# Storing the first 120 sums of each partition early and the last 8 late, in a row-sum kernel at the end of a stream of loads

## The chip, the cores and the metric

One core of one Trainium2 chip runs the whole program. The metric is the time of one execution on the device in microseconds (us), the median over several executions. The profile is one execution taken by the hardware profiler; its times count from the start of the span. The span leaves out about 2.0 us of the measured time. Engines are TensorE (PE), VectorE (DVE), ScalarE (ACT), GpSimd (POOL) and SyncE (SP), which issues the transfers. A transfer of the kernel has one descriptor (the order to move one piece) for each partition, and the trace shows each piece as a packet. A transfer has landed when the last of the 16 DMA engines has raised its semaphore. The receipt is the time from the end of an engine's last packet to that signal.

## The reference

```python
def setup_inputs():
    batch, seq, dim = 32, 512, 1024
    return {"x": np.abs(np.random.randn(batch, seq, dim)).astype(np.float32) + 1e-6}

def reference(x):
    return np.sum(1.0 / x, axis=-1).astype(np.float32)
```

There are 16384 rows of 1024 numbers. Each of the 128 partitions gets 128 rows, so the result is a tile of 128 partitions by 128 columns of float32: 512 bytes for each partition, 64 KB in all.

## The kernel before

Loads of x (64 MB) stream through a ring of 40 rows. A row is handled as two halves a and b, since 1/a + 1/b = (a + b)/(ab): products on GpSimd or VectorE, reciprocals as exp(-ln) on ScalarE, half sums on TensorE, and the multiplication with the sum over the row on VectorE, whose result goes to one column of `sums`. The last 24 rows follow a fixed order, in which `T119` means "sum of row 119"; `W127` and `X127` handle row 127 on ScalarE alone.

```python
    LAST = 104
    LAST_LOADS = [2] * 1 + [4] * 1 + [2] * 5 + [1] * 8
    ORDER = """
        ... E116 S118 V118 E117 P120 T115 L118+
        P121 S119 T116 E118+ T117 P122 L120+ S122 T118 E120+ D123 L122+ T120
        S123 P124 E122+ T119 D125 S125 L124 T122 L125 P126 T121 E124 S126 E125
        T123 L126 T124 W127 E126 T125 X127 T126
    """
    # ... cut: the pools, the main loop over rows 0 to 103, the loads of the last rows ...
    for op in order:
        # ... cut: the other kinds of operation ...
        elif kind == "X":
            keep(nc.scalar.activation(out=rows, in_=rows, func=Exp, scale=-1.0,
                                      accum_out=sums[:, c : c + 1]))

    nc.sync.dma_start(out=out_v, in_=sums)
```

The transfers are numbered in the order of their issue: 31 loads, then the store as the 32nd. Each signals its completion on one of eight semaphores, used in turn. At its end SyncE waits for eleven semaphores: the eight, and one each of GpSimd, ScalarE and VectorE.

## Time and profile before

| quantity | value |
|---|---|
| time, median of 6 runs (those taken with the changed kernel included) | 169.22 us (169.12 to 169.84) |
| span of the profiled run | 167.1 us |
| the one store: issue, in us from the start | 164.767 |
| issue to last landing | 1.537 us |
| last landing to the end of the span | 0.834 us |

The lines of the page that carry this, and how they are read, stand in the prediction below. One more is needed later, from the view of the program's end (L286): how often SyncE's queue ran a semaphore instruction there, with the shortest, median and longest duration in ns, and when the first and the last began.

```profile
L286 SPq EVENT_SEMAPHORE  x7: 17/28/28, 165.2 to 167.1; - x7
```

Five of these seven are the waits for the eleven semaphores (a drain carries the eleventh), two belong to the barrier, in which the engines wait for one another. The wait for the store is not inside a record here. In these traces a record begins once the first semaphore that the instruction names is there: the fifth instruction names the store's semaphore first and began at 166.320, 0.016 us after the landing.

### The profile page before, as it was taken

Reading aid. Unit: us, or ns where it says so; the run is one execution under the profiler, and the core shown is the slowest. Engines: PE = TensorE matmul, PEld = TensorE weight load, DVE = VectorE, ACT = ScalarE, POOL = GpSimd, SP = SyncE. Lnnn points to the kernel's source line nnn. Section 1 sums busy time; section 2 is a strip of 40 time slices with the busy share of each in tenths; the row PEclk is TensorE's granted clock in tenths of the full one; section 3 lists DMA queues with packets and bytes.
Section 4 is the critical chain, followed back from the end, with each engine's and each line's share of the span. In section 5 each row is a group of like instructions: output and inputs, shape, how many; then the busy total and the mean of one; then the engine's idle time right before and its main releaser. Section 6 shows DMA issues by size and latency. Waiting matters only on the chain.

```text
span 167.1 us, 1139 instructions
## 1 busy us (share of the span) xinstructions
PE 108.6 (65%) x204; PEld 43.0 (26%) x204; DVE 135.6 (81%) x272; ACT 133.9 (80%) x137; POOL 130.2 (78%) x73
## 2 busy tenths in 40 slices
PE   0007946193864919179471935926999996998990
PEld 0003321040321303033221302402444442433430
DVE  0001797979979798998979897898699999998994
ACT  3002888979788797878979785999899999999994
POOL 1007969698895969979696985999999997999630
PEclk9999999969789699957999696985899999999999
DMA  6999999999999999999999999999999999999910
GB/s 204 423 439 439 431 439 416 447 408 463 408 441 431 439 439 431 431 418 439 416 439 431 447 396 416 427 422 431 433 423 414 433 420 422 418 416 410 409 64 18
DMA packets 4614, 67.23 MB, mean 402 GB/s; under 512 B 512, under 2 KB 640, under 8 KB 1664
## 3 DMA queue, kind: packets, MB, share of 16 engines
q1 hardware_dynamic: 4608, 67.18, 94.7%
q14 instruction: 5, 0.04, 0.1%
q8 instruction: 1, 0.02, 0.0%
HBM read 67.11 MB, written 0.07 MB: 402 GB/s over the span
## 4 chain that ended last, share of the span: by engine, by line
DMA 67%; POOL 12%; ACT 7%; issue 6%; DVE 4%; SPq 1%; PE 1%; ACTq 1%; POOLq 0%
DMA ring<-in_x_dram 67%; POOL pr L158 12%; ACT pr L230 3%; DVE ring L109 2%; ACT pr L236 2%; DVE pr L109 2%; SPq L139 1%; ACT r L236 1%; PE bb L99 1%; ACT pr L169 1%; ACT ring L248 1%; ACT r L174 1%; ACTq L286 1%; DVE pr L221 0%; DVE sums L109 0%
## 5 line engine op out<-in xcount | busy, mean ns | idle before, releaser
L158 POOL TENSOR_TENSOR pr<-ring 128x1024 f32<-128x1024 f32 (+1 forms) x52 | 107.2, 2102 | 26.6 <-DMA ring<-in_x_dram 24.2
L99 PE MATMUL s<-ring,ident 128*128 128x512 f32 x172 | 89.5, 669 | 5.8 <-DVE sums L109 5.5
L169 ACT ACTIVATE pr<-pr 128x1024 f32<-128x1024 f32 x52 | 54.7, 1051 | 27.8 <-POOL pr L158 27.1
L109 DVE CUSTOM_DVE_ANT_1 pr<-ring,r 128x1024 f32<-128x1024 f32 x40 | 48.8, 1221 | 10.2 <-ACT r L174 9.8
L109 DVE CUSTOM_DVE_ANT_1 ring<-ring,r 128x1024 f32<-128x1024 f32 x44 | 53.4, 1216 | 0.0
L99 PEld LDWEIGHTS s<-ring,ident 128*128 128x128 f32 x172 | 36.8, 218 | 58.7 <-issue 41.2
L99 PE MATMUL b<-ring,ident 128*128 128x512 f32 x26 | 19.0, 820 | 46.8 <-DMA ring<-in_x_dram 46.8
L174 ACT ACTIVATE r<-pr 128x1024 f32<-128x1024 f32 x36 | 37.0, 1028 | 1.1
L109 DVE CUSTOM_DVE_ANT_0 pr<-pr,s 128x512 f32<-128x512 f32 x43 | 27.9, 682 | 0.0
L212 POOL TENSOR_TENSOR pr<-ring 128x512 f32<-128x512 f32 (+1 forms) x15 | 22.3, 1500 | 4.2 <-DMA ring<-in_x_dram 2.5
L147 DVE TENSOR_TENSOR pr<-ring,b 128x512 f32<-128x512 f32 x13 | 8.9, 685 | 18.5 <-PE b L99 18.5
L99 PEld LDWEIGHTS b<-ring,ident 128*128 128x128 f32 x26 | 5.2, 238 | 56.2 <-DMA ring<-in_x_dram 37.8
L179 ACT ACTIVATE pr<-pr 128x1024 f32<-128x1024 f32 x16 | 16.9, 1058 | 0.5
L230 ACT ACTIVATE pr<-pr 128x1024 f32<-128x1024 f32 (+1 forms) x14 | 12.4, 899 | 0.5 <-DVE pr L221 0.3
L109 DVE DVE_READ_ACCUMULATOR2_ANT sums<- 128x1 f32 x127 | 10.5, 83 | 0.0
L236 ACT ACTIVATE r<-pr 128x1024 f32<-128x1024 f32 (+1 forms) x8 | 6.4, 806 | 0.1
L236 ACT ACTIVATE pr<-pr 128x1024 f32<-128x1024 f32 (+1 forms) x7 | 6.0, 863 | 0.1
L99 PE MATMUL bb<-ring,ident 128*128 128x512 f32 x6 | 3.4, 644 | 2.0 <-DMA ring<-in_x_dram 1.2
L221 DVE TENSOR_TENSOR pr<-ring,bb 128x512 f32<-128x512 f32 x3 | 2.1, 685 | 0.3 <-PE bb L99 0.2
L99 PEld LDWEIGHTS bb<-ring,ident 128*128 128x128 f32 x6 | 0.9, 188 | 4.5 <-DMA ring<-in_x_dram 2.8
L70 ACT ACT_TABLE_LOAD x1 | 1.3, 1283 | 0.7 <-PEq L275 0.7
L214 DVE TENSOR_TENSOR pr<-ring 128x512 f32<-128x512 f32 x2 | 1.4, 687 | 0.0
(9 smaller groups left out, 3.2 us busy)
## 6 DMA issues: line engine op xcount, KB each, us to landing
ring<-in_x_dram SPq DMA_DIRECT2D x10, 4096.0 KB, 37.1
ring<-in_x_dram SPq DMA_DIRECT2D x7, 2048.0 KB, 35.7
ring<-in_x_dram SPq DMA_DIRECT2D x6, 1024.0 KB, 30.8
ring<-in_x_dram SPq DMA_DIRECT2D x8, 512.0 KB, 14.4
out_dram<-sums SPq DMA_DIRECT2D x1, 64.0 KB, 1.5
```

Of the source, the lines that this page charges most:

```text
L99: i = nc.tensor.matmul(bank, lhsT=ident, rhs=half, start=k == 0, stop=k == len(halves) - 1,)
L109: i = nc.vector.tensor_tensor_reduce(out=row if out is None else out, in0=row, in1=fac, scale=S, scalar=0.0, op0=mult, op1=plus, accum_out ...
L139: keep(nc.sync.dma_start(out=xt, in_=x_v[:, c0 : c0 + n, :]))
L147: i = nc.vector.tensor_tensor(out=pr[:, j, :], in0=xt[:, q + j, :H], in1=b, op=mult)
L158: i = nc.gpsimd.tensor_tensor(out=pr[:, v:, :], in0=xc[:, v:, :H], in1=xc[:, v:, H:], op=mult)
L169: keep(nc.scalar.activation(out=pr, in_=pr, func=Ln, scale=S))
L174: nc.scalar.activation(out=r, in_=pr[:, e:, :], func=Exp, scale=-1.0)
L179: keep(nc.scalar.activation(out=r, in_=r, func=Exp, scale=-1.0))
L212: keep(nc.gpsimd.tensor_tensor(out=pr, in0=a, in1=b, op=mult))
L221: nc.vector.tensor_tensor(out=pr[:, 0, :], in0=a[:, 0, :], in1=bs[c], op=mult)
L230: keep(nc.scalar.activation(out=pr, in_=pr, func=Ln, scale=S))
L236: keep(nc.scalar.activation(out=r, in_=pr, func=Exp, scale=-1.0))
```

## The change

The intent is to take most of the store's bytes off the end: 120 of 128 columns are complete some 5 us before the last one, so they can leave while the last rows are still computed, and only 4 KB are left for the end.

```diff
+    STORED = 120
...
+    left = set(range(LAST, F))
     for op in order:
...
-
-    nc.sync.dma_start(out=out_v, in_=sums)
+        if kind in "TX":
+            left.discard(c)
+            if c < STORED and min(left) >= STORED:
+                keep(
+                    nc.sync.dma_start(out=out_v[:, :STORED], in_=sums[:, :STORED])
+                )
+
+    assert not left
+    nc.sync.dma_start(out=out_v[:, STORED:], in_=sums[:, STORED:])
```

## The prediction

> **What bounds the kernel now.** I read the page's first lines first, then the slices, then the tail in the timeline and the waits of SyncE's queue, because the change touches nothing but how the sums leave the chip.
>
> ```profile
> span 167.1 us, 1139 instructions
> DMA  6999999999999999999999999999999999999910
> GB/s 204 423 439 439 431 439 416 447 408 463 408 441 431 439 439 431 431 418 439 416 439 431 447 396 416 427 422 431 433 423 414 433 420 422 418 416 410 409 64 18
> DMA 67%; POOL 12%; ACT 7%; issue 6%; DVE 4%; SPq 1%; PE 1%; ACTq 1%; POOLq 0%
> ```
>
> For 38 of 40 slices the loads of x run at some 420 GB/s, and the chain of waits puts 67% of the span on them. That part is not touched. The last two slices (a slice is 4.2 us) are a tail: the last row's arithmetic, then the one store of all sums, then the end of the program. What the change can move is there alone. The timeline of the tail:
>
> ```profile
> 158.66 0.68 DVE L109 CUSTOM_DVE_ANT_0 pr<-pr,s 128x512 f32<-128x512 f32 x1
> 159.27 0.08 DVE L109 DVE_READ_ACCUMULATOR2_ANT sums<- 128x1 f32 x1
> ...
> 164.56 0.19 ACT L251 ACTIVATION_READ_ACCUMULATOR ring<-ring 128x1 f32 x1
> 164.59 0.08 DVE L109 DVE_READ_ACCUMULATOR2_ANT sums<- 128x1 f32 x1
> 164.77 0.34 SPq L260 DMA_DIRECT2D out_dram<-sums  x1
> ```
>
> The last sum of VectorE (row 126) is there at 164.59 + 0.08 = 164.67, the one of ScalarE (row 127) at 164.56 + 0.19 = 164.75 (164.74 unrounded), and the store is issued at 164.77, hence behind ScalarE. The first two lines are the sum of row 119: in the program's order it is the last of rows 0 to 119, so 120 columns are there at 159.35. Between are 5.4 us in which a store could leave. Then the list of DMA issues and the waits of SyncE's queue:
>
> ```profile
> out_dram<-sums SPq DMA_DIRECT2D x1, 64.0 KB, 1.5
> SPq L260 <- DVE sums L109: 13.0, 1, 13.0
> SPq L286 <- DMA out_dram<-sums: 0.9, 1, 0.9
> ```
>
> From issue to landing the store takes 1.5 us, and the end of the program (L286) waits 0.9 us of them. So the exposed end is 164.77 to 167.14, some 2.4 us. I took it apart from the trace's records of single packets and of SyncE's sequencer (us from the start): issue 164.767 to 165.110 (0.343); first packet 165.606; 128 packets of 512 bytes, about 27 ns each, and the 16 small ones that raise the semaphore, the last ending at 165.965; last landing seen at 166.304; SyncE's next instruction at 166.320; last instruction of the barrier ends at 167.138. Measured time (169.21) is 2.1 us above the span and stays so.
>
> **What the Trainium skill says.** (1) "DMA: Bandwidth & Descriptors", section "Anatomy of one DMA", puts a fixed cost of about 2 us on a transfer, most of it the receipt of the write and nearly none of it its bytes. The trace agrees in kind: of 1.54 us (164.767 to 166.304) only 0.36 are packets; 0.84 lie before the first and 0.34 behind the last. (2) The same page, "Measured", has 0.68 us of DMA busy time for 4 KB and 0.95 us for 64 KB (loads, issued by GpSimd), a difference of 0.27; those are just the sizes of the late store and of the old one, but here all 64 KB took 0.36, so I size the gain from the packets instead. (3) Its "Specifications" say that pieces under 512 bytes make the DMA read, modify and write. The old store has 512 bytes for each partition, the new ones 480 and 32. No record of before shows this. (4) "Queues, rings and completion order" says that an engine takes the descriptors of one ring in order; so the early store, issued by SyncE like the loads, goes behind the loads that are still queued. The last data packet of the loads ends at 160.95; the trace of before has nothing to test this.
>
> **The change part by part.** Comparing the order of instructions on each engine, PE, DVE, ACT and POOL have the same instructions with the same waits; SyncE has one transfer more. In particular DVE's later sums do not wait for the early store, since it reads other columns.
>
> *Early store, 120 columns.* It waits for the sum of row 119 (159.35) and for an old load; issue takes some 0.34 us, first packet at the earliest 159.4 + 0.84 = 160.2, behind the loads by 161.0, landed by about 161.6, more than 3 us ahead of the late store's issue. The DMA is idle from 161 on. All of it lies beside VectorE's and ScalarE's arithmetic: cost 0. Gain also 0 of itself, since another store is still to come.
>
> *Late store, 8 columns.* It waits for the same last sums of ScalarE and VectorE, so it is issued at 164.77 as before. It has still 128 descriptors, one for each partition. Issue is the same whatever their size: the loads with 4096 bytes for each took 0.327 us (SyncE's records), this one 0.343. The 0.50 us from the end of the issue to the first packet and the 0.34 us of receipt stay. What falls is the packet time: a load packet of 4096 bytes took 159 ns and one of 512 bytes 27 ns, so (159 - 27) / 3584 = 0.037 ns for each byte; 32 bytes would take 27 - 480 x 0.037, about 9 ns, which is also what the 4-byte semaphore packets took. An engine's share is 8 packets: 8 x 27 = 0.216 us becomes 8 x 9 = 0.072, a gain of at most 0.14. Since the engines begin staggered as descriptors come, I take 0.10. This is an estimate.
>
> *The end.* This is a cost that the diff does not show. SyncE's last instruction waits for eleven semaphores: GpSimd, ScalarE, VectorE and eight that the transfers use in turn. It is built as five semaphore instructions of two waits each and a drain. In the trace of before the first four stand at 165.156, 165.220, 165.282 and 165.346, 63 ns apart, long before the store lands; only the fifth holds the store's semaphore (the eighth in turn, as the store is the 32nd transfer), begins at 166.320, and the drain follows 65 ns later. In the changed program the early store takes the eighth, the late store, the 33rd transfer, the first one in turn. By the order of the semaphores in the records, its wait sits in the third instruction. So the fourth and the fifth come behind the landing: 2 x 0.063 = 0.13 us more.
>
> *Pieces of 32 bytes.* If writing less than 512 bytes to HBM costs a read before, the receipt gets longer. Guess: 0 to 0.2, I take 0.03, as most of the 0.34 is a round trip anyway.
>
> Sum: - 0.10 + 0.13 + 0.03 = + 0.06 us on 169.21, hence 169.25: within noise of nothing.
>
> **The rivals.** *The store's time is by bytes*: then cutting 64 KB to 4 KB would take most of the packet phase and perhaps more away. For it: the intent of the change, and the skill's 0.27 us. Against: only 0.36 us of the exposed 2.4 are packets. At best 169.21 - 0.36 = 168.85, which is 0.2%. *Small writes are slow*: 128 pieces of 32 bytes[...]. For it: the skill's specification. Against: one such read is short beside 0.34 us and the 16 engines do theirs side by side. If each of an engine's 8 packets waited for a round of some 0.2 us in sequence, it would be + 1.6 us, 170.8; I give that 3 in 100. *The early store delays the last loads or VectorE*: for it, loads run until 160.95 and the early store's issue falls at 159.4. Against: ring order, and no new wait on any compute engine. It would cost less than 0.2 us, and the last load has slack: it landed at 161.40 and ScalarE read its row at 162.14.
>
> **Range and chances.** The three runs of before go from 169.12 to 169.84, so noise of 0.3 us covers every term of the sum. 168.9 to 169.7 holds the sum's own uncertainty (- 0.2 to + 0.3) and most of that noise. For 2% the time would have to move by 3.4 us. The whole exposed end is 2.4 us, so faster by that much is all but impossible (1 in 100, for a chance of another kind); slower is so only if small writes are bad beyond anything in the trace (1 in 100).
>
> **What would show it.** In the changed profile: two stores, the early one issued near 159.4, the late one at 164.8 with an issue of 0.34; packets of about 9 ns, over in some 0.25 us where it was 0.36; landing 1.4 to 1.5 us after issue (1.5 before); and from landing to the end of the span 0.96 us where it was 0.83 (167.138 - 166.304). If the late store lands in well under 1.3 us, the first rival is right; if in over 1.7, the second; if the late store is issued after 165.0 or the last loads land later, the third. A wait of VectorE for the early store would make the prediction wrong, and would show as DVE idle after 159.4.

## The result, and the profile after

The changed kernel took 169.37 us, median of 6 runs (169.01 to 169.53), against 169.22 us of the kernel before. Ratios here are the mean time of one kernel's fast runs over that of the other's of the same rounds, so not quite the ratio of the medians. This one is 1.0001, with a 95% interval from 0.9983 to 1.002: the same. The time lies inside the predicted range.

From the page of the changed kernel: the span, the chain of waits by engine, and the two stores with KB and us from issue to landing.

```profile
span 167.5 us, 1141 instructions
...
DMA 52%; ACT 17%; PE 13%; DVE 6%; POOL 4%; issue 4%; SPq 1%; ACTq 1%; POOLq 0%
...
out_dram<-sums SPq DMA_DIRECT2D x1, 60.0 KB, 1.8
out_dram<-sums SPq DMA_DIRECT2D x1, 4.0 KB, 1.4
```

The late store has a sixteenth of the bytes of the old one and lands 1.4 us after its issue instead of 1.5. The chain's shares have moved from DMA to ACT and PE, but not as an effect of the early store: the same kernel run again had DMA 61% and PE 3%, and the variants below have from 52% to 78% for DMA.

The tail in the timeline of the changed kernel (start, duration, engine, line, operation):

```profile
159.09 0.68 DVE L111 CUSTOM_DVE_ANT_0 pr<-pr,s 128x512 f32<-128x512 f32 x1
159.70 0.08 DVE L111 DVE_READ_ACCUMULATOR2_ANT sums<- 128x1 f32 x1
...
159.81 0.35 SPq L266 DMA_DIRECT2D out_dram<-sums  x1
...
164.93 0.18 ACT L254 ACTIVATION_READ_ACCUMULATOR ring<-ring 128x1 f32 x1
165.02 0.08 DVE L111 DVE_READ_ACCUMULATOR2_ANT sums<- 128x1 f32 x1
165.16 0.34 SPq L270 DMA_DIRECT2D out_dram<-sums  x1
```

The early store follows the sum of row 119 at once. VectorE and ScalarE go on as before. The late store is issued 0.05 us after ScalarE's last sum (0.03 before), so it waits for nothing new. But all of it is 0.40 us later than in the kernel before: 165.16 against 164.77. That shift is already there at the sum of row 119 (159.09 against 158.66), before the early store has been issued. Whether it is scatter was left to the experiments.

The waits of SyncE's queue, and the semaphore instructions of the end in the changed kernel:

```profile
SPq L266 <- DVE sums L111: 7.2, 1, 7.2
SPq L270 <- DVE sums L111: 5.0, 1, 5.0
...
SPq L296 <- DMA out_dram<-sums: 0.9, 1, 0.9
```

```profile
L296 SPq EVENT_SEMAPHORE  x7: 17/28/913, 165.6 to 167.5; - x7
```

The wait at the end is 0.9 us, just as before, although the store lands earlier after its issue. The second fence shows why the landing is not the end of it. One of the seven instructions lasted 913 ns. By the records of SyncE's sequencer it is the third of the five, it began at 165.679 and ended at 166.592, with the landing at 166.570. The fourth (166.629), the fifth (166.691) and the drain (166.756) come after it. In the kernel before only the fifth (166.320) and the drain (166.385) followed the landing at 166.304.

From the records of single packets and of the sequencer, the end of both kernels in us, each column from an event to the next:

| kernel | issue to first packet | first to last packet's end | to last landing | issue to landing | landing to end | issue to end |
|---|---|---|---|---|---|---|
| before | 0.839 | 0.359 | 0.339 | 1.537 | 0.834 | 2.371 |
| changed | 0.837 | 0.203 | 0.366 | 1.406 | 0.944 | 2.350 |

The packets gained 0.156, the last receipt ("to last landing") lost 0.027 and the end lost 0.110. Of the exposed end 0.021 us are left, 0.01% of the time.

### The profile page after: what moved, and what is told of

Same layout as the page of the kernel before. It is cut to its first block, busy times and chain, and to the rows that moved or that the text cites. A ratio compares the mean times of both kernels' runs of the same rounds, so it can differ in the third digit from the quotient of the medians.

```text
span 167.5 us, 1141 instructions
## 1 busy us (share of the span) xinstructions
PE 108.8 (65%) x204; PEld 43.4 (26%) x204; DVE 135.6 (81%) x272; ACT 133.5 (80%) x137; POOL 130.1 (78%) x73
## 4 chain that ended last, share of the span: by engine, by line
DMA 52%; ACT 17%; PE 13%; DVE 6%; POOL 4%; issue 4%; SPq 1%; ACTq 1%; POOLq 0%
DMA ring<-in_x_dram 52%; PE s L101 11%; ACT pr L233 6%; POOL pr L160 4%; ACT r L239 3%; ACT pr L239 3%; DVE ring L111 3%; DVE pr L111 3%; ACT pr L171 2%; PE b L101 2%; SPq L141 1%; ACT r L176 1%; ACT pr L181 1%; ACTq L296 1%; ACT ring L251 1%
## 5 line engine op out<-in xcount | busy, mean ns | idle before, releaser
L101 PE MATMUL s<-ring,ident 128*128 128x512 f32 x172 | 88.6, 664 | 5.2 <-DVE sums L111 5.2
L101 PE MATMUL b<-ring,ident 128*128 128x512 f32 x26 | 20.4, 876 | 47.9 <-DMA ring<-in_x_dram 47.9
```

Of the source, the lines that this page charges most:

```text
L101: i = nc.tensor.matmul(bank, lhsT=ident, rhs=half, start=k == 0, stop=k == len(halves) - 1,)
```

## The experiments

My theory was: (a) the packets of the late store are shorter by their bytes alone; (b) the time from landing to end depends on which of the eight semaphores the late store happens to use, since the last wait names them in a fixed order, and not on the store's size; (c) the 0.40 us are scatter of the main loop. Rivals are given with each run. What an edit does to the times is 0.1 us in 169, so the traces decide and the times only confirm that nothing large happened. The runs with one look are of state unknown; for them only the intervals at the end are used, which repeat to some 0.01 us. Their times are given here once and carry no argument: 169.55 us (late store alone) and 169.44 (one column early), beside 169.57 for the kernel before on that chip; 170.23 (three pieces), 170.15 (halves), 169.96 (early on GpSimd) and 169.30 (late on ScalarE) on a second chip, beside a single 169.29.

**The changed kernel again** (no edit).

> The changed kernel once more, unedited, for the scatter of the trace. In its first trace the late store was issued at 165.16 us, 0.40 later than in the kernel before, though the delay was there before the early store left (VectorE's sum of row 120 began at 157.95 instead of 157.51, the early store was issued at 159.81). My theory: that 0.40 is scatter of the main loop; issue of the late store falls anywhere from 164.6 to 165.4 here, and from the issue on things repeat to 0.02 us: 1.41 from issue to last landing, 0.94 from landing to the end of the span, ratio of times 1.000 plus or minus 0.002. Rival (the second transfer delays the arithmetic): late store issued at 165.1 to 165.2 again, and the ratio is 1.002.

```profile
164.54 0.19 ACT L254 ACTIVATION_READ_ACCUMULATOR ring<-ring 128x1 f32 x1
164.57 0.08 DVE L111 DVE_READ_ACCUMULATOR2_ANT sums<- 128x1 f32 x1
164.76 0.34 SPq L270 DMA_DIRECT2D out_dram<-sums  x1
```

In this timeline the late store is issued at 164.76, which is where the kernel before had its only one. The early store was there and the late one was not delayed, so part (c) holds. Issue to landing was 1.413, landing to end 0.944. The times were 169.87 us (169.06 to 170.28, 6 runs) against 169.57 us (169.14 to 170.69, 11 runs) of the kernel before on the same chip, ratio 1.0014 (0.9981 to 1.0047): the same.

**The late store alone** (wrong result, columns 0 to 119 are never written).

```diff
-                keep(
-                    nc.sync.dma_start(out=out_v[:, :STORED], in_=sums[:, :STORED])
-                )
+                pass
```

> Wrong result on purpose: the early store is left out, only the 8 last columns are stored. The late store is then the 32nd transfer and uses the same semaphore in turn as the one store of the kernel before. My theory (the small store gains 0.13 us by its packets, and loses 0.11 to the place of its semaphore in the last wait): issue to landing 1.41 as in the changed kernel, landing to end 0.83 as in the kernel before, 2.24 together. Rival A (small pieces, not the place of the semaphore, make the end longer): landing to end 0.94. Rival B (the early store delays the late one's issue by 0.4): issue back at 164.77 or below; by mine it is anywhere from 164.6 to 165.4.

```profile
165.27 0.34 SPq L268 DMA_DIRECT2D out_dram<-sums  x1
```

```profile
L294 SPq EVENT_SEMAPHORE  x7: 17/28/28, 165.7 to 167.4; - x7
```

No instruction at the end is long here. Issue to landing 1.408, landing to end 0.834, together 2.242. With the old semaphore the small store has the old end, so small pieces do not lengthen it. The late store was issued at 165.27, even later than in the first run of the changed kernel, with no early store at all: rival B falls once more.

**One column early, all columns late.**

```diff
-                    nc.sync.dma_start(out=out_v[:, :STORED], in_=sums[:, :STORED])
+                    nc.sync.dma_start(out=out_v[:, :1], in_=sums[:, :1])
...
-    nc.sync.dma_start(out=out_v[:, STORED:], in_=sums[:, STORED:])
+    nc.sync.dma_start(out=out_v, in_=sums)
```

> The reverse: the early store takes one column only, just so that it uses up the 32nd place, and the late store takes all 128 columns again (512 bytes for each partition), with the first semaphore in turn. My theory: issue to landing 1.54 as in the kernel before, landing to end 0.94 as in the changed kernel, 2.48 together, 0.11 worse than before and the worst of all variants. It waits for one semaphore more ahead of its issue, which may add 0.06 there. Rival A (small pieces make the end longer): landing to end 0.83. Rival C (the landing depends on there being two stores): landing well off 1.54.

The late store's timeline and the semaphore instructions of the end:

```profile
164.86 0.34 SPq L270 DMA_DIRECT2D out_dram<-sums  x1
```

```profile
L296 SPq EVENT_SEMAPHORE  x7: 17/28/1053, 165.2 to 167.3; - x7
```

The large store now has the long end: an instruction of 1053 ns, again the third. Issue to landing was 1.546, landing to end 0.939, together 2.485. It was issued 0.025 us after ScalarE's last sum, so the additional wait cost nothing. With the runs so far, size and place of the semaphore have been crossed, and each acts on its own interval only:

| late store | semaphore named in the fifth instruction | in the third |
|---|---|---|
| 512 bytes for each partition | 1.537 + 0.834 | 1.546 + 0.939 |
| 32 bytes | 1.408 + 0.834 | 1.406 + 0.944 |

**Eight early pieces**, so that the late store is the 40th transfer and uses the eighth semaphore as the old store did.

```diff
-                keep(
-                    nc.sync.dma_start(out=out_v[:, :STORED], in_=sums[:, :STORED])
-                )
+                for q in range(0, STORED, STORED // 8):
+                    e = q + STORED // 8
+                    keep(nc.sync.dma_start(out=out_v[:, q:e], in_=sums[:, q:e]))
```

> The early store is cut into eight of 15 columns each, so that the late store is the 40th transfer and gets the same semaphore in turn as the one store of the kernel before. If my theory holds, this has the gain without the loss: issue to landing 1.41, landing to end 0.83, 2.24 together, 0.11 better than the changed kernel and 0.13 better than the kernel before; in the times that is 0.07%, inside the interval. The eight issues of 0.34 us each take 2.8 us beside the arithmetic and all must have landed before the late store lands, at most by 164.5. Rival D (eight issues in a row hold up SyncE or the transfers): late store issued over 0.1 us behind the last sum, or landing over 1.5 us after issue.

```profile
SPq L267 <- DMA ring<-in_x_dram: 7.3, 8, 1.0
SPq L270 <- DVE sums L111: 2.7, 1, 2.7
...
SPq L296 <- DMA out_dram<-sums: 0.4, 1, 0.4
```

```profile
L296 SPq EVENT_SEMAPHORE  x7: 17/28/28, 165.4 to 167.2; - x7
```

The long instruction is gone. Issue to landing was 1.401, landing to end 0.835, together 2.236: 0.114 less than the changed kernel and 0.135 less than the kernel before. This version takes the gain without the loss. Rival D falls: the late store was issued 0.025 us behind ScalarE's last sum. I had pictured the eight pieces wrongly: six of them are issued before row 119 is summed (at 159.65 in this run; the sixth piece went at 159.28), because each waits only for the columns it carries and for the last user of its semaphore, a load (the first line: eight waits for loads). The last was issued at 161.9. The 0.4 in the third line is not a shorter wait for the landing: the third instruction began only at 165.961, 0.455 us after the second and not 0.06, though the last of its semaphores was up at 163.223. Why is open; it costs nothing, since the landing came at 166.457. The pieces are not quite free either: the last load landed 1.396 us behind the one before it, against 1.238 in the kernel before. The slack before ScalarE reads that row took this up. The times were 169.43 us (169.32 to 169.66, 6 runs) against 169.57 us, ratio 0.9992 (0.9967 to 1.0018): the same, as 0.08% cannot be seen.

**Three early pieces**: the same edit with 3 in place of 8. (The expectation calls the late store the 34th transfer; behind 31 loads and three pieces it is the 35th, which is the third semaphore in turn, as it says.)

```diff
-                keep(
-                    nc.sync.dma_start(out=out_v[:, :STORED], in_=sums[:, :STORED])
-                )
+                for q in range(0, STORED, STORED // 3):
+                    e = q + STORED // 3
+                    keep(nc.sync.dma_start(out=out_v[:, q:e], in_=sums[:, q:e]))
```

> The early store in three pieces of 40 columns, so that the late one (still 8 columns) is the 34th transfer and takes the third semaphore in turn, which the last wait of SyncE names in its first of five instructions, not in the third (changed kernel) or the fifth (kernel before). My theory: four instructions now follow the landing, each 0.063 us, so landing to end is 0.834 + 4 x 0.063 = 1.09 us; issue to landing stays 1.41; 2.49 together, 0.12 worse than the kernel before although it stores the same 8 columns late. Rival (landing to end has only two values, 0.83 with the old semaphore and 0.94 with any other): 0.94.

```profile
L296 SPq EVENT_SEMAPHORE  x7: 17/28/1050, 166.2 to 168.3; - x7
```

The long instruction is now the first one (it began at 166.177), and four follow. Issue to landing was 1.405, landing to end 1.087, together 2.492: from issue to end the 8 late columns take longer than all 128 did in the kernel before. The place of the semaphore has more than two values. In detail, the drain came 0.312 us after the landing, against 0.186 in the changed kernel and 0.081 before, so four and two more instructions cost 0.231 and 0.105: 0.063 each, less 0.021, since the instruction that is already waiting reacts sooner: it ended 0.022 us behind the landing in the changed kernel and 0.023 here, while the fifth of the kernel before ended 0.044 behind. That leaves 0.022 of the 1.087, of which 0.017 is that SyncE itself left the last barrier behind the others. So the expected 1.09 was hit in part by luck: the four instructions cost 0.02 less than expected and the barrier 0.02 more.

**Halves**: 64 columns early, 64 late.

```diff
-                    nc.sync.dma_start(out=out_v[:, :STORED], in_=sums[:, :STORED])
+                    nc.sync.dma_start(out=out_v[:, :64], in_=sums[:, :64])
...
-    nc.sync.dma_start(out=out_v[:, STORED:], in_=sums[:, STORED:])
+    nc.sync.dma_start(out=out_v[:, 64:], in_=sums[:, 64:])
```

> The changed kernel with halves: 64 columns early, 64 late, hence 256 bytes for each partition in both. My sum for the packets: 27 - 256 x 0.037 = 17.5 ns for each packet; the last data packet ends halfway between 1.19 (512 bytes) and 1.03 us (32 bytes) after the issue, at 1.11; with the longer receipt seen for 32 bytes (0.357 against 0.334) issue to landing is 1.48; landing to end 0.94 (first semaphore in turn). Rival (pieces below 512 bytes all cost a read before the write, the more so the more bytes are not whole lines): receipt 0.40 or more.

Packets took 18 ns, the last data packet ended 1.101 us after the issue, issue to landing was 1.459 (1.48 expected) and landing to end 0.939. The other runs' early stores lie on the same line: 26 ns for 480 bytes, 14 for 160, 11 for 60. The typical receipt (median over the 16 engines, with packets and signals each put in order of time, since the trace does not name the engines) was 0.340, against 0.334 with 512 bytes in the kernel before and 0.357 with 32 in the changed one; three early pieces, also 32 bytes, had 0.383. So whatever a piece of under 512 bytes costs besides is some 0.02 to 0.05 us at most here, far from what the rival needs, and the rival falls.

**The early store on GpSimd.**

```diff
-                    nc.sync.dma_start(out=out_v[:, :STORED], in_=sums[:, :STORED])
+                    nc.gpsimd.dma_start(out=out_v[:, :STORED], in_=sums[:, :STORED])
```

> The early store is issued by GpSimd instead of SyncE, behind its last product. It then counts among GpSimd's own transfers, and the late store is the 32nd on SyncE, with the old semaphore. My theory: issue to landing 1.41, landing to end 0.83, 2.24 together, the same as with eight early pieces but with two transfers only; the last wait names twelve semaphores, one more, which costs at most one 0.063 us instruction ahead of the landing, if the old semaphore still stands in the last instruction. Rival (a transfer of GpSimd has to be drained at the end at some cost of its own): landing to end above 0.90.

```profile
160.50 0.71 POOL L266 DMA_DIRECT2D out_dram<-sums  x1 [0.57 <-DVE sums L111]
161.23 1.29 POOL L215 TENSOR_TENSOR pr<-ring 128x512 f32<-128x512 f32 x1
```

Against the expectation the store went in front of GpSimd's last product, and its issue took 0.71 us there. The product began 0.23 us after its load had landed (161.000), where it was 0.13 in all nine other traces. ScalarE's last sum came 0.16 us behind VectorE's, where it was 0.01 to 0.08 in the others. So this place seems to cost some 0.09 us of the arithmetic, by one trace, which the intervals from the issue on do not contain. Issue to landing was 1.411, landing to end 0.893, together 2.304. The drain followed the landing by 0.084 us as in the kernel before, so the old semaphore did its part. But the barrier behind it took 0.06 us longer: GpSimd's clearing of the semaphores took 0.139 us instead of 0.096, and its two drains 0.089 and 0.040 instead of 0.078 and 0.034. Neither expectation fits exactly: the rival's direction is right, its size too large. Whether it is the twelfth semaphore or GpSimd's own transfer that costs this is open.

**The late store on ScalarE.**

```diff
-    nc.sync.dma_start(out=out_v[:, STORED:], in_=sums[:, STORED:])
+    nc.scalar.dma_start(out=out_v[:, STORED:], in_=sums[:, STORED:])
```

> The late store is issued by ScalarE, the engine that makes the last sum, and not by SyncE. In the kernel before 0.026 us lie between ScalarE's end and SyncE's issue. My theory: that hop is all there is to gain, and ScalarE still waits for VectorE's last sum and its own; issue 0.02 to 0.10 us behind its last accumulator read; issue to landing 1.41 as for SyncE, landing to end 0.94. Rival (ScalarE's own way to the transfers is slower or faster): issue to landing off by more than 0.1 us.

```profile
164.74 0.18 ACT L254 ACTIVATION_READ_ACCUMULATOR ring<-ring 128x1 f32 x1
...
164.95 0.37 ACTq L270 DMA_DIRECT2D out_dram<-sums  x1
```

It is issued 0.030 us after ScalarE's last accumulator read, so nothing is gained at the hop. The issue itself took 0.370 us instead of 0.343, issue to landing was 1.439, landing to end 0.938, together 2.377: 0.02 to 0.03 worse than on SyncE.

**Spans that differ more than the edits do.** Three of these eight runs had spans of 168.0 to 168.3 us, all from the second set of runs, on the second chip (the fourth run of that set and the kernel before on that chip had 167.3). Their second load had its last packet at 23.3 us, while the other seven traces, the kernel before included, had it at 22.5 to 22.7. The 31 loads are the same in all kernels and no store has begun by then, so this is not an effect of the edits. It is not the only delay: the late store alone was 0.50 us late with its second load on time (its last load landed at 161.90, against 161.40 before), and the changed kernel was 0.40 us late with its last load on time (161.44). Where these come from was not pursued.

## Why the prediction was right

The predicted 169.25 us and the measured 169.37 us differ by less than the runs among themselves, so the time says only that no term was large. It could not tell the predicted + 0.06 from the measured - 0.02. (Two slips in the prediction: 169.21 + 0.06 is 169.27, not 169.25; and the loads run at some 420 GB/s in 37 slices, as the first has 204.) More to the point are the steps.

- **The early store costs nothing.** Confirmed: no new wait on any compute engine, VectorE busy as before, and the late store's issue at 164.76 in the repeat. It landed by 161.6 (159.81 + 1.8), as estimated. The last load landed at 161.44 and in the repeat at 161.39, against 161.40 before. That a store goes behind the queued loads is borne out by the runs whose first store was issued earlier: in halves it was issued at 153.32 and its first packet began at 159.71, with eight pieces at 152.84 and 159.01, hence 6.2 to 6.4 us later and not 0.84. For the changed kernel's own early store it cannot be seen: its first packet began at 160.66, 0.85 us after the issue, and the last load packet ended at 160.99, on which engines the trace does not tell.
- **The late store's issue does not shrink.** Confirmed: 0.343 us again, and 0.837 us to the first packet against 0.839.
- **Packets.** Confirmed in mechanism, mis-sized: the packets took 9 ns as worked out, but the phase from first to last shrank by 0.156 us, where I took 0.10 and allowed at most 0.14. The 0.01 beyond that bound is not explained by a run.
- **Small pieces.** I guessed + 0.03 for a longer receipt; the last landing came 0.027 later after its packet, the typical one 0.023. That is luck, as nothing in the trace of before bore on it.
- **The place of the semaphore.** Confirmed, and by three places rather than two. The term was 0.13 and measured 0.110, because the instruction that is already waiting reacts 0.02 us sooner than one that has yet to begin.
- **The sum.** - 0.10 + 0.13 + 0.03 = + 0.06 was predicted; - 0.156 + 0.027 + 0.110 = - 0.02 was measured at the end of the span. The sign was wrong, at a size that no timing shows.
- **The rivals.** The store by its bytes had its ceiling at 0.36 us and would have reached 0.13 of it (late store alone). Small writes being slow is excluded at the size that it had (halves, and the receipts of 0.36 to 0.38 us). The early store delaying the arithmetic is excluded for SyncE (the repeat, and the delay without an early store).

The gain of about 0.13 us from the smaller last store is thus real, though it is read from the traces alone and no timing here shows it. All but 0.02 of it was given back by the last wait, because one more transfer moved the late store to another semaphore.

## What to carry to other kernels

This last store of 64 KB was mostly fixed time: of the 2.37 us from its issue to the end, 0.36 were packets, and splitting it shortened only those. Before building such a split, take the interval from issue to end apart and see which piece goes with the bytes. And where an edit adds or removes a transfer, look at which semaphore the last transfer then gets and where the final wait names it: here each instruction behind it cost 0.06 us, and with three early pieces that was more than the edit gained.

## What the Trainium skill lacked or had wrong

- "DMA: Bandwidth & Descriptors", section "Measured", has 0.68 us of DMA busy time for 4 KB and 0.95 us for 64 KB (loads issued by GpSimd). The stores of SyncE here took 0.20 us and 0.36 us from the first packet to the end of the last; the difference is 0.16, not 0.27. No page has these times for stores by SyncE.
- The same page, "Anatomy of one DMA", gives a fixed cost of about 2.0 us for GpSimd's path, most of it the receipt, and no fit for a small store by SyncE, to which the prediction carried it over. Here 4 KB landed 1.41 us after the issue and 64 KB after 1.54, of which 0.84 lie before the first packet and 0.34 to 0.37 behind the last. So for these stores by SyncE the part before the data was larger than the receipt.
- Its "Specifications" warn of a read-modify-write below 512 bytes. For a store of 128 pieces of 32 bytes the receipt was 0.357 us (0.383 in one run) instead of 0.334 with 512 bytes, and the packets were shorter (9 ns instead of 27). The page does not say what the warning costs a small store; here it was at most 0.05 us.
- No page says that the wait for all semaphores at the end of a program is a row of instructions of two waits each, 0.063 us apart, so that the landing-to-end time depends on the semaphore of the last transfer: 0.83 us (fifth instruction), 0.94 (third) and 1.09 (first).
